# Forming the product of a row's minimum score and the row's scale on the scalar engine instead of the vector engine

## The chip, the cores and the metric

The kernel runs on one core of one Trainium2 chip. The metric is the device time of one execution in microseconds, lower is better. Three timed executions of the kernel before gave 1954.22, 1947.15 and 1951.80 us, median 1951.8 us. The engines are named as the profile names them: PE is the matrix engine (PEld its weight loads), DVE the vector engine, ACT the scalar engine, POOL the GpSimd engine, SP the queue that issues DMAs. Each engine works through its own instructions in the order in which they stand, and waits for the others through semaphores.

## The reference, cut to what matters

Two layers of a trunk over 512 latent tokens and 256 context tokens, D_MODEL 1024, all in float32. Each layer projects the normalised tokens, runs two kinds of attention (a 2-D neighbourhood attention with 8 heads, and a grouped-query attention with 8 query heads over 2 key heads), merges the two branches with gates, and runs a gated feed-forward block. The change touches the softmax of the grouped-query attention alone, and there the query's own normalisation:

```
def rms_norm(x, g):
    xf = x.astype(jnp.float32)
    y = xf * lax.rsqrt(jnp.mean(xf * xf, axis=-1, keepdims=True) + EPS)
    return (y * g.astype(jnp.float32)).astype(x.dtype)

qb = apply_rope(rms_norm(heads(gq, GQA_Q_HEADS), q_gain[l]), cos, sin)
kb = apply_rope(rms_norm(heads(gk, GQA_KV_HEADS), k_gain[l]), cos, sin)

def softmax_attn(q, k, v):
    s = jnp.einsum('bgrqd,bgkd->bgrqk', q, k).astype(jnp.float32) * SCALE
    p = jax.nn.softmax(s, axis=-1).astype(v.dtype)
    return jnp.einsum('bgrqk,bgkd->bgrqd', p, v)
```

## The kernel before, in words

Every float32 product is done in three passes of a faster number format: each operand is split into a high and a low part (high by a copy on ACT, low by a subtraction on DVE or POOL), and PE multiplies high by high, high by low and low by high. So nearly every tile costs ACT and DVE an operation each, and PE three matmuls.

The query is not normalised before its scores are formed. The scores come out of PE with the sign turned (QSCALE is negative), and the factor 1/rms of a query row, `r`, is applied inside the softmax: the exponential is exp(nr * s + m), where `nr` is -r (one number a row) and `m` is r times the smallest (most negative) score of the row. So the softmax needs three steps before its exponential: the smallest score of each row (L1048, a reduction on DVE over 768 scores), its product with `r` (L1054), and the exponential on ACT with `m` as bias and `nr` as scale (L1056), which also sums the row. Behind it DVE takes the reciprocal of the sum (L1009) and scales the row (L1010). PE then turns the probabilities (tile `tp`, L1066), ACT and DVE split them (`pth` L1016, `ptl` L1017), PE multiplies them with the values (tile `y`, L1076), and ACT and DVE join its two halves (`ys` L1024, L1027).

`gqa_pair` makes an item of one head and two blocks of 128 queries: `scores` for both, then `soft` for both, then `exp` for both, then three calls of `turn`, then `values`. There are 16 such items in each layer, 64 softmaxes of 128 rows by 768 keys in all. `ctx_item` does the same for the context queries (layer 0 only): two blocks side by side, 256 keys each; for the grouped-query heads (8 of 16) it forms the products of both blocks at L1098.

What sets the order. In the attention part PE's order is written out by a planner, `Flow`: it keeps a clock of PE and a line of booked time for ACT ("a"), DVE ("v") and POOL ("g"). `go` books an operation at the first gap of its engine's line, at fixed rates (table RATE: an "a" operation 0.06 us and 0.00083 us a column, a "v" operation 0.065 us and 0.00105 us a column, times a factor of the layer), and returns when its result is there. The items are PE's main thread; between their steps, while a result is not yet due, the planner lets PE work on fillers: the projections that are still to be done (tile `pj`, L384, and `pv`, L957). When a `turn` may stand in PE's order is what `go` returned for its `exp`. The scores have one PSUM buffer for an item (`sc`, one of three banks), so the next item's scores wait for both exponentials; `tp` and `y` share three banks. The order on ACT, DVE, POOL and SP is set by a scheduler that follows its own model of times, with PE's order as given.

Of the kernel before, what the change touches and what calls it, by code (L numbers as in the profile page):

```python
# [14 lines left out]
AF = mybir.ActivationFunctionType  # L15
ALU = mybir.AluOpType
# [9 lines left out]
T = S + CTX  # L26
# [308 lines left out]
class Trunk:  # L335
# [694 lines left out]
    def gqa_pair(self, head, q, kk, val, out, i, pool, done=None):  # L1030

        nc = self.nc
        qt, r, nr, v = q
        ps_, pts = [], []

        def scores(s, b):

            for lo, up in ((0, S), (S, T)) if b % 2 == 0 else ((0, 256), (256, T)):
                for k in range(2):
                    nc.tensor.matmul(  # L1040
                        s[:, lo:up], qt[:, b * P : (b + 1) * P], kk[k][:, lo:up],
                        start=(k == 0 and (b % 2 == 0 or lo > 0)), stop=(k == 1), skip_group_check=True)

        ms = {}

        def soft(s, b, at):
            m = ms[b] = pool.tile([P, 2], F32, tag="m", bufs=4, name=self.name("m"))
            nc.vector.tensor_reduce(m[:, 0:1], s[:, :T], axis=AX.X, op=ALU.min)  # L1048
            return self.go(("v", T), at=at)

        def exp(s, b, at):
            m = ms[b]
            c = 2 * b + v
            nc.vector.tensor_tensor(m[:, 0:1], m[:, 0:1], r[:, c : c + 1], op=ALU.mult)  # L1054
            p = pool.tile([P, T], F32, tag="p", name=self.name("p"))
            nc.scalar.activation(p, s[:, :T], AF.Exp, bias=m[:, 0:1], scale=nr[:, c : c + 1], accum_out=m[:, 1:2])  # L1056
            self.soften(p, m[:, 1:2], pool)
            ps_.append(p)
            end = self.go(("v", 1), ("e", T), at=at)
            return end, self.go(("v", 1), ("w", T), at=end)  # L1060

        def turn(k):
            tp = self.ps("t", "tp")
            for b in range(2):
                for j in range(2):
                    nc.tensor.transpose(  # L1066
                        tp[:, (2 * j + b) * P : (2 * j + b + 1) * P], ps_[b][:, (k + j) * P : (k + j + 1) * P], self.ident)
            pts.append(self.split_t(tp, pool))
            return self.go(("a", S), ("v", S), at=self.flow.clock + 4 * PASS)

        def values():
            y = self.ps("b", "y")
            for hl in range(2):
                for k in range(6):
                    j = k % 2
                    nc.tensor.matmul(  # L1076
                        y[:, 0:256], val[:, k * P : (k + 1) * P], pts[k // 2][hl][:, j * 256 : (j + 1) * 256],
                        start=(hl == 0 and k == 0), stop=(hl == 1 and k == 5))
            return self.join(y, out, head, [(0, 256, 256 * i)], pool)

        return Item(
            [(lambda s, b=b: scores(s, b), lambda s, at, b=b: soft(s, b, at), lambda s, at, b=b: exp(s, b, at))
             for b in (2 * i, 2 * i + 1)], T,
            [lambda k=k: turn(k) for k in (0, 2, 4)], [values],
            (2 * T * COL, 4 * PASS, 12 * 256 * COL), done)

    def ctx_item(self, head, score, val, out, r, nr, v, pool, done):

        nc = self.nc
        ps_, pts = [], []  # L1090

        def soft(s, at):
            m = pool.tile([P, 4], F32, tag="mc", bufs=4, name=self.name("m"))
            nc.vector.tensor_reduce(
                m[:, 0:2], s[:, 0:512].rearrange("p (a b) -> p a b", a=2), axis=AX.X, op=ALU.min)
            if r is not None:
                rr = r[:].rearrange("p (t v) -> p v t", v=2)[:, v, 4:6]
                nc.vector.tensor_tensor(m[:, 0:2], m[:, 0:2], rr, op=ALU.mult)  # L1098
            p = pool.tile([P, 512], F32, tag="p", name=self.name("p"))
            for b in range(2):  # L1100
                c = slice(b * 256, (b + 1) * 256)
                scale = -1.0 if nr is None else nr[:, 8 + 2 * b + v : 9 + 2 * b + v]
                nc.scalar.activation(
                    p[:, c], s[:, c], AF.Exp, bias=m[:, b : b + 1], scale=scale, accum_out=m[:, 2 + b : 3 + b])
                self.soften(p[:, c], m[:, 2 + b : 3 + b], pool)
            ps_.append(p)
            end = self.go(("v", S), ("v", 1), ("e", 256), ("e", 256), at=at)
            return end, self.go(("v", 1), ("v", 1), ("w", 256), ("w", 256), at=end - 0.5)

        def turn():  # L1110
            p = ps_[0]
            tp = self.ps("t", "tp")
            for k in range(2):
                for b in range(2):
                    nc.tensor.transpose(
                        tp[:, (2 * k + b) * P : (2 * k + b + 1) * P],
                        p[:, b * 256 + k * P : b * 256 + (k + 1) * P], self.ident)
            pts.append(self.split_t(tp, pool))
            return self.go(("a", S), ("v", S), at=self.flow.clock + 4 * PASS)

        def values():
            y = self.ps("b", "y")
            for hl in range(2):
                for k in range(2):
                    nc.tensor.matmul(
                        y[:, 0:256], val[:, (4 + k) * P : (5 + k) * P], pts[0][hl][:, k * 256 : (k + 1) * 256],
                        start=(hl == 0 and k == 0), stop=(hl == 1 and k == 1))
            return self.join(y, out, head, [(0, 256, S)], pool)

        return Item([(score, soft)], 512, [turn], [values], (4 * 256 * COL, 4 * PASS, 4 * 256 * COL), done)  # L1130

    def gqa_ctx(self, head, q, kk, val, out, pool, done=None):
# [1225 lines left out]
```

## Time and profile before

| What | Value |
|---|---|
| median of three timed runs | 1951.8 us (1947.15 to 1954.22) |
| the profiled execution | 1945.29 us, its span 1943.5 us, so 1.79 us around the span |
| busy share of the span | PE 98%, PEld 91%, DVE 76%, ACT 49%, POOL 12% |
| granted PE clock, mean | 0.998 of full speed |
| the exponentials of the items in layer 0 | 97 to 264 us of the span |
| the exponentials of the items in layer 1 | 1193 to 1316 us of the span |

A matmul's row in the trace is longer than its share of PE, since matmuls overlap: what PE needs for one is the distance between two starts. PE is at work in nearly all of the span, so time can be lost or won only where PE stands idle or runs at a lower clock, and the views that tell this are the waits of PE and the busy time by stretch.

### The profile page before, as it was taken

Reading aid. Unit: us, or ns where it says so; the run is one execution under the profiler, and the core shown is the slowest. Engines: PE = TensorE matmul, PEld = TensorE weight load, DVE = VectorE, ACT = ScalarE, POOL = GpSimd, SP = SyncE. Lnnn points to the kernel's source line nnn. Section 1 sums busy time; section 2 is a strip of 40 time slices with the busy share of each in tenths; the row PEclk is TensorE's granted clock in tenths of the full one; section 3 lists DMA queues with packets and bytes.
Section 4 is the critical chain, followed back from the end, with each engine's and each line's share of the span. In section 5 each row is a group of like instructions: output and inputs, shape, how many; then the busy total and the mean of one; then the engine's idle time right before and its main releaser. Section 6 shows DMA issues by size and latency. Waiting matters only on the chain.

```text
span 1943.5 us, 31493 instructions
## 1 busy us (share of the span) xinstructions
PE 1912.1 (98%) x12298; PEld 1775.8 (91%) x12298; DVE 1470.0 (76%) x2802; ACT 943.0 (49%) x1822; POOL 226.6 (12%) x131
## 2 busy tenths in 40 slices
PE   8999999999999999999999998999999999999998
PEld 8989999998899999999999888889988999999998
DVE  7468887769877888786868577888657687877785
ACT  5466666652336533342424346666553355544553
POOL 0332222213300000000000012322300000000000
PEclk9999999999999999999999999999999999999999
DMA  8121112235562233334344411112235532332332
GB/s 328 44 65 48 47 64 63 77 105 182 170 217 87 66 120 122 117 116 133 131 141 143 143 62 55 47 60 64 73 102 173 201 109 77 98 120 88 103 97 83
DMA packets 71669, 210.85 MB, mean 108 GB/s; under 512 B 8544, under 2 KB 10720, under 8 KB 71520
## 3 DMA queue, kind: packets, MB, share of 16 engines
q1 hardware_dynamic: 71520, 208.84, 33.5%
q8 instruction: 96, 1.57, 0.3%
q14 instruction: 53, 0.43, 0.1%
HBM read 196.75 MB, written 6.82 MB: 105 GB/s over the span
## 4 chain that ended last, share of the span: by engine, by line
PE 69%; DVE 4%; issue 1%; ACT 1%; POOL 0%; DMA 0%; DVEq 0%; POOLq 0%; ACTq 0%
PE po L384 21%; PE qu L1740 14%; PE pj L384 11%; PE qv L1740 7%; PE pp L384 4%; PE qc L1740 3%; PE pf L384 3%; PE pv L957 1%; PE sc L1040 1%; PE y L1076 1%; PE tp L1066 1%; PE y L1203 1%; PE sc L1167 1%; PE tp L1191 1%; DVE m L1048 0%
## 5 line engine op out<-in xcount | busy, mean ns | idle before, releaser
L1740 PE MATMUL qu<-r,w 128*128 128x384 f32 (+1 forms) x1872 | 295.9, 310 | 0.3
L1740 PEld LDWEIGHTS qu<-r,w 128*128 128x128 f32 x1872 | 281.0, 190 | 4.9 <-DVE tt L2219 3.7
L384 PE MATMUL pj<-h,wh 128*128 128x512 f32 (+1 forms) x704 | 257.4, 366 | 3.3 <-ACT kg L816 1.7
L384 PE MATMUL pj<-h,wl 128*128 128x512 f32 (+1 forms) x704 | 247.6, 352 | 1.2 <-POOL wl L371 1.2
L384 PE MATMUL pj<-hl,wh 128*128 128x512 f32 (+1 forms) x704 | 247.0, 351 | 0.0
L369 ACT ACTIVATE wh<-wr 128x1024 fp32r<-128x1024 f32 (+1 forms) x131 | 124.6, 954 | 168.9 <-issue 43.5
L1603 ACT ACTIVATE w<-wr 128x512 fp32r<-128x512 f32 x234 | 145.4, 625 | 107.6 <-DVE wr L2183 36.1
L384 PE MATMUL po<-ph,wh 128*128 128x512 f32 (+1 forms) x576 | 197.5, 343 | 0.0
L384 PE MATMUL po<-ph,wl 128*128 128x512 f32 (+1 forms) x576 | 196.9, 342 | 0.0
L384 PE MATMUL po<-pl,wh 128*128 128x512 f32 (+1 forms) x576 | 196.3, 341 | 0.0
L371 POOL TENSOR_TENSOR wl<-wr,wh 128x1024 fp32r<-128x1024 f32 (+1 forms) x67 | 151.0, 2258 | 370.8 <-ACT wh L369 364.7
L1595 DVE SCALAR_TENSOR_TENSOR x<-po,G,x 128x256 f32<-128x256 f32 (+3 forms) x168 | 99.2, 596 | 101.0 <-PE po L384 100.0
L1607 DVE TENSOR_TENSOR w<-wr,w 128x512 fp32r<-128x512 f32 x234 | 159.4, 686 | 11.9 <-ACT w L1603 11.0
L384 PEld LDWEIGHTS pj<-h,wl 128*128 128x128 f32 x704 | 133.3, 189 | 19.7 <-POOL wl L371 1.6
L1740 PE MATMUL qv<-r,w 128*128 128x384 f32 (+1 forms) x936 | 150.7, 310 | 0.3 <-ACT tt L1746 0.3
L384 PEld LDWEIGHTS pj<-h,wh 128*128 128x128 f32 x704 | 133.7, 190 | 17.4 <-ACT kg L816 1.9
L384 PEld LDWEIGHTS pj<-hl,wh 128*128 128x128 f32 x704 | 134.0, 190 | 13.5
L1740 PEld LDWEIGHTS qv<-r,w 128*128 128x128 f32 x936 | 141.2, 190 | 0.5 <-ACT tt L1746 0.5
L1016 ACT ACTIVATE pth<-tp 128x512 fp32r<-128x512 f32 x176 | 103.2, 595 | 65.1 <-PE tp L1066 36.8
L512 POOL TENSOR_TENSOR rs<-rs,expo 128x2 f32<-128x2 f32 (+2 forms) x8 | 6.2, 773 | 1100.4 <-DVE rs L511 1100.4
L1017 DVE TENSOR_TENSOR ptl<-tp,pth 128x512 fp32r<-128x512 f32 x176 | 119.4, 684 | 18.4 <-ACT pth L1016 17.0
L384 PEld LDWEIGHTS po<-ph,wl 128*128 128x128 f32 x576 | 108.3, 188 | 14.3 <-DVE wl L1911 0.4
(255 smaller groups left out, 4325.2 us busy)
## 6 DMA issues: line engine op xcount, KB each, us to landing
wr<-wfi SPq DMA_DIRECT2D x88, 512.0 KB, 3.3
wr<-wmodT SPq DMA_DIRECT2D x84, 512.0 KB, 3.4
wr<-win SPq DMA_DIRECT2D x68, 512.0 KB, 3.3
wr<-wfo SPq DMA_DIRECT2D x64, 256.0 KB, 2.7
wr<-wo SPq DMA_DIRECT2D x26, 512.0 KB, 3.9
wr<-wp SPq DMA_DIRECT2D x32, 256.0 KB, 3.0
x<-x SPq DMA_DIRECT2D x16, 384.0 KB, 6.7
wr<-wmod SPq DMA_DIRECT2D x12, 512.0 KB, 7.6
```

The lines of the kernel that those rows point to most:

```text
L369: nc.scalar.activation(hi, raw, AF.Copy)
L371: (eng or nc.gpsimd).tensor_tensor(lo, raw, hi[:].bitcast(F32), op=ALU.subtract)
L384: nc.tensor.matmul(ps[:, : b - a], u[:, c], v[k][:, a:b], start=(k == 0 and i == 0), stop=(k == nk - 1 and i == 2),)
L957: nc.tensor.matmul(ps[:, t * 256 : t * 256 + 256], a[k][:, tok], b[:, c], start=(k == 0 and i == 0), stop=(k == KB - 1 and i == 2))
L1016: nc.scalar.activation(hi, tp, AF.Copy)
L1017: nc.vector.tensor_tensor(lo, tp, hi[:].bitcast(F32), op=ALU.subtract)
L1040: nc.tensor.matmul(s[:, lo:up], qt[:, b * P : (b + 1) * P], kk[k][:, lo:up], start=(k == 0 and (b % 2 == 0 or lo > 0)), stop=(k == 1), ski ...
L1066: nc.tensor.transpose(tp[:, (2 * j + b) * P : (2 * j + b + 1) * P], ps_[b][:, (k + j) * P : (k + j + 1) * P], self.ident)
L1595: self.nc.vector.scalar_tensor_tensor(x[j][:, f:u], ps[:, f - a : u - a], self.G[l][i][:, s, j : j + 1], x[j][:, f:u], op0=ALU.mult, op1=A ...
L1603: self.nc.scalar.activation(t[:, :n], src, AF.Copy)
L1607: self.nc.vector.tensor_tensor(t[:, n : 2 * n], src, t[:, :n].bitcast(F32), op=ALU.subtract)
L1740: nc.tensor.matmul(banks[bank], u[:, c], v, start=(first and k == 0 and i == 0), stop=(k == kn - 1 and i == 2), skip_group_check=True)
```

## The change

At two places the small product moves from DVE to ACT. In `exp` one multiplication of a column of 128 numbers becomes one ACT activation (a copy with the row's scale as factor). In `ctx_item` one DVE multiplication of two columns becomes two ACT activations of one column. In `exp` the planner's booking of one column changes from "v" to "a"; the booking in `ctx_item` stays.

```
-            nc.vector.tensor_tensor(m[:, 0:1], m[:, 0:1], r[:, c : c + 1], op=ALU.mult)
+            nc.scalar.activation(m[:, 0:1], m[:, 0:1], AF.Copy, scale=r[:, c : c + 1])
             p = pool.tile([P, T], F32, tag="p", name=self.name("p"))
             nc.scalar.activation(p, s[:, :T], AF.Exp, bias=m[:, 0:1], scale=nr[:, c : c + 1], accum_out=m[:, 1:2])
...
-            end = self.go(("v", 1), ("e", T), at=at)
+            end = self.go(("a", 1), ("e", T), at=at)
             return end, self.go(("v", 1), ("w", T), at=end)
...
-                nc.vector.tensor_tensor(m[:, 0:2], m[:, 0:2], rr, op=ALU.mult)
+                for b in range(2):
+                    nc.scalar.activation(m[:, b : b + 1], m[:, b : b + 1], AF.Copy, scale=rr[:, b : b + 1])
```

DVE has 72 instructions fewer (64 and 8), ACT 80 more (64 and 16). The number of ACT's table loads is four as before, and DMAs are as many as before. Because the planner books another line, orders change too, all of it inside the two attention stages; behind them each engine has the instructions of before in the order of before.

On ACT, in layer 0, around the exponentials of the second item (first the order before: `pth` are high parts of turned probabilities, `qh` high parts of a projection, `p` the exponentials):

```order
L1016 ACTIVATE pth_1078<-tp_1073 128x512
L1016 ACTIVATE pth_1087<-tp_1082 128x512
L1016 ACTIVATE pth_1096<-tp_1091 128x512
L990 ACTIVATE qh_1103<-pj_1026 64x448
L1056 ACTIVATE p_1062,m_1057<-sc_1048,m_1057,nr_778 128x768
L1056 ACTIVATE p_1068,m_1059<-sc_1048,m_1059,nr_778 128x768
```

The same place on ACT with the change:

```order
L1016 ACTIVATE pth_1078<-tp_1073 128x512
L1054 ACTIVATE m_1057<-m_1057,hr_775 128x1
L1016 ACTIVATE pth_1087<-tp_1082 128x512
L1016 ACTIVATE pth_1096<-tp_1091 128x512
L1056 ACTIVATE p_1062,m_1057<-sc_1048,m_1057,nr_778 128x768
L1054 ACTIVATE m_1059<-m_1059,hr_775 128x1
L990 ACTIVATE qh_1103<-pj_1026 64x448
L1056 ACTIVATE p_1068,m_1059<-sc_1048,m_1059,nr_778 128x768
```

The first product stands two copies ahead of its exponential, the second between the two exponentials with a copy of a projection behind it, which stood ahead of both before.

On PE, in layer 0, the third turn of the same item (its exponentials are p_1062 and p_1068) beside a projection that fills PE's time; a piece of the difference:

```order
 L384 MATMUL pj_1212<-h_127,wl_1024 128x512
+L1066 MATMUL tp_1225<-ident_sb,p_1062 128x128 x2
+L1066 MATMUL tp_1225<-ident_sb,p_1068 128x128 x2
 L384 MATMUL pj_1212<-h_129,wh_1022 128x512
 L384 MATMUL pj_1212<-hl_130,wh_1022 128x512
 L384 MATMUL pj_1212<-h_129,wl_1024 128x512
-L1066 MATMUL tp_1228<-ident_sb,p_1062 128x128 x2
-L1066 MATMUL tp_1228<-ident_sb,p_1068 128x128 x2
```

The turn stands three matmuls of a filler earlier. Counted over both layers, 61 of the items' 96 turns stand behind fewer columns of projections than before, by up to 9216 columns (18 matmuls of 512), two behind more, and the rest as before.

On DVE, in layer 1, around the reductions of the item whose scores follow the first evacuation of a key projection `k` there (the order before):

```order
L1017 TENSOR_TENSOR ptl_13250<-tp_13244,pth_13249 128x512
L936 TENSOR_TENSOR k_13321<-pj_13168,k_13321 64x512
L1048 TENSOR_REDUCE m_13271<-sc_13262 128x1
L1048 TENSOR_REDUCE m_13273<-sc_13262 128x1
L936 TENSOR_TENSOR k_13324<-pj_13168,k_13324 64x512
L1054 TENSOR_TENSOR m_13271<-m_13271,hr_12267 128x1
L1017 TENSOR_TENSOR ptl_13293<-tp_13287,pth_13292 128x512
L1054 TENSOR_TENSOR m_13273<-m_13273,hr_12267 128x1
L1027 TENSOR_TENSOR y_13221<-y_13296,ys_13309 64x256
```

The same place on DVE with the change:

```order
L1017 TENSOR_TENSOR ptl_13332<-tp_13326,pth_13331 128x512
L936 TENSOR_TENSOR k_13338<-pj_13245,k_13338 64x512
L936 TENSOR_TENSOR k_13341<-pj_13245,k_13341 64x512
L1048 TENSOR_REDUCE m_13367<-sc_13358 128x1
L1048 TENSOR_REDUCE m_13369<-sc_13358 128x1
L1017 TENSOR_TENSOR ptl_13389<-tp_13383,pth_13388 128x512
L1027 TENSOR_TENSOR y_13198<-y_13392,ys_13405 64x256
```

The two products are gone from the queue, and the low parts of `k` now stand together ahead of both reductions that follow them; `ptl` stands behind the reductions as before.

## Rows read from the trace of the kernel before

**Rows 1.** The page's busy time: us, share of the span, instructions.
```profile
PE 1912.1 (98%) x12298; PEld 1775.8 (91%) x12298; DVE 1470.0 (76%) x2802; ACT 943.0 (49%) x1822; POOL 226.6 (12%) x131
```

**Rows 2.** By stretch: length, busy us of PE, PEld, DVE, ACT, POOL; clock, DMA.
```profile
94.00:200.00 106.00, 104.17 (x691) 94.41 (x690) 79.31 (x170) 65.39 (x133) 31.13 (x14) 1.00 0.17 52
200.00:300.00 100.00, 100.00 (x693) 92.22 (x692) 86.09 (x180) 66.49 (x139) 23.05 (x14) 1.00 0.19 58
300.00:416.00 116.00, 114.32 (x843) 107.30 (x842) 83.87 (x225) 70.63 (x176) 26.61 (x16) 1.00 0.25 75
1190.00:1320.00 130.00, 123.57 (x809) 110.05 (x808) 103.76 (x220) 83.96 (x163) 30.84 (x17) 0.99 0.13 40
1320.00:1440.00 120.00, 119.56 (x843) 110.52 (x842) 87.27 (x220) 71.43 (x160) 32.79 (x19) 1.00 0.26 77
```

**Rows 3.** PE's waits over the span: total us, times, longest us.
```profile
PE sc L1040 <- ACT p L1056: 2.0, 2, 1.7
PE tp L1066 <- DVE ptl L1017: 1.9, 1, 1.9
...
PE y L1076 <- DVE ptl L1017: 1.6, 3, 0.8
...
PE tp L1066 <- DVE p L1010: 0.8, 1, 0.8
```

**Rows 4.** Lines 1054 and 1098: min/median/max ns, and who waited for L1054.
```profile
L1054 DVE TENSOR_TENSOR m<-m,hr x64: 140/150/2060, 97.0 to 1315.5; 128x1 f32<-128x1 f32 x64
...
  ACT p L1056: 21.1, 18
...
L1098 DVE TENSOR_TENSOR m<-m,hr x8: 147/157/1886, 129.4 to 271.7; 128x2 f32<-128x2 f32 x8
```

**Rows 5.** ACT's groups by shape: busy us, mean ns, idle before.
```profile
L990 ACT ACTIVATE qh<-pj 64x64 fp32r<-64x64 f32 x16 | 3.4, 215 | 3.2 <-DVE ql L991 3.0
...
L815 ACT ACTIVATE sq<-pj 128x256 f32<-128x256 f32 x6 | 2.2, 370 | 0.0
...
L816 ACT ACTIVATE qg<-pj,qgain 128x256 f32<-128x256 f32 x4 | 1.9, 474 | 0.0
```

**Rows 6.** Timeline, layer 0's second item: start us, us, engine, line, operation.
```profile
104.30 1.82 DVE L1048 TENSOR_REDUCE m<-sc 128x1 f32<-128x768 f32 x2 [1.47 <-PE sc L1040]
...
105.65 0.39 PE L384 MATMUL pj<-hl,wh 128*128 128x512 f32 x1
...
105.88 0.40 PE L384 MATMUL pj<-h,wl 128*128 128x512 f32 x1
...
106.11 1.28 DVE L1017 TENSOR_TENSOR ptl<-tp,pth 128x512 fp32r<-128x512 f32 x2
...
107.31 0.15 DVE L1054 TENSOR_TENSOR m<-m,hr 128x1 f32<-128x1 f32 x1
...
107.72 0.98 ACT L1056 ACTIVATE p<-sc,m,nr 128x768 f32<-128x768 f32 x1
...
109.42 0.62 DVE L1010 TENSOR_SCALAR p<-p,rc 128x768 f32<-128x768 f32 x1
...
110.37 0.60 PE L1066 MATMUL tp<-ident_sb,p 128*128 128x128 f32 x4
```

**Rows 7.** Timeline, layer 1's first item.
```profile
1189.34 1.81 DVE L1048 TENSOR_REDUCE m<-sc 128x1 f32<-128x768 f32 x2
...
1191.30 1.28 ACT L1056 ACT_TABLE_LOAD   x1 [5.45 <-DVE m L1054]
...
1194.87 0.50 PE L1040 MATMUL sc<-kk,q 128*128 128x512 f32 x1 [1.67 <-ACT p L1056]
```

**Rows 8.** Timeline, layer 1, PE's longest wait between items.
```profile
1284.69 0.66 PE L1066 MATMUL tp<-ident_sb,p 128*128 128x128 f32 x4 [1.91 <-DVE ptl L1017]
```

**Rows 9.** The stretch behind that wait, as rows 2.
```profile
1286.00:1288.00 2.00, 2.00 (x10) 1.80 (x9) 1.64 (x4) 0.49 (x1) 0.00 (x0) 0.50 0.00 0
```

**Rows 10.** Waits of all engines, POOL's for the neighbourhood bias buffers.
```profile
POOL bias L1491 <- DVE m L1178: 50.5, 6, 14.7
```

## The prediction

> **What bounds the kernel now.** I read the page's busy times first. PE is at work in 98% of the span, DVE in 76% [rows 1]: the matmuls bound the kernel, and the change leaves every one of them in place, so it can only add or remove time in which PE stands still. Next I read the attention stages by stretch, since the products run from 97.0 to 1315.5 us [rows 4] and the orders differ only inside the two attention stages. The length of a stretch less PE's busy time is what PE lacks there: 1.8, 0, 1.7, 6.4 and 0.4 us, together 10.4 us [rows 2]. DVE is the next busiest engine there (79.3 of 106, 86.1 of 100, 103.8 of 130 us where the grouped-query items run), ACT is third (65.4, 66.5 and 84.0) [rows 2]. Then PE's waits: for the exponential 2.0 us in two waits, for `ptl` 1.9 us in one, for `ptl` ahead of `y` 1.6 us in three, for the scaled row 0.8 us in one [rows 3]. No wait of PE names the product itself. ACT's does: it waited 21.1 us in 18 waits for L1054 [rows 4], but nearly all of that lies beside PE's fillers. Last I read one item in the timeline, to see what distance there is between a softmax and the turn that needs it.
>
> **What goes from DVE.** 64 products of 150 ns and 8 of 157 ns [rows 4]: 9.6 + 1.3 = 10.9 us of DVE time. On the path it is worth far less, since PE waits for DVE in so few places. What each product also costs is its place in the queue. In the second item both reductions end at 104.30 + 1.82 = 106.12 us, and the second product starts only at 107.31, because two `ptl` subtractions, a merged 1.28 us that begins at 106.11, stand ahead of it; its exponential starts at 107.72 [rows 6].
>
> **What comes to ACT.** 80 activations of one column with a scale taken from a tile. The trace shows none. Nearest is a copy of 64x64 at 215 ns; 256 columns take 370 ns, so a column costs (370 - 215) / 192 = 0.8 ns and one column alone about 215 - 51 = 164 ns. A scale taken from a tile costs 474 - 370 = 104 ns [rows 5]. The estimate is 164 + 104 = 268 ns, with bounds of 150 (no dearer than on DVE) and 215 + 104 = 319 ns. I take 0.27: 80 x 0.27 = 21.6 us of ACT time (12.0 to 25.5). ACT has idle time for it: in 130 us of layer 1 it was busy for 84.0 [rows 2], and 32 products there add 8.6.
>
> The Trainium skill, "ScalarE: Activation LUTs", section "What ACT_TABLE_LOAD costs", gives an ACTIVATE 186 ns and 0.833 ns a column, and about 93 ns more for each operand of one column. That is 280 ns here as an estimate, and the 104 ns of the row agree with its 93; by it the ACT term would be 22.4 us. It speaks against the change: the product is nearly twice as dear on ACT. The same section says that ACTIVATEs back to back overlap by about 93 ns; an exponential that waits for a product on its own engine would lose that, 64 x 0.093 = 6.0 us more of ACT, which no run here shows yet.
>
> **How long a softmax takes.** On the path of one item the first product needs the first reduction alone, which ends near 104.30 + 0.91 = 105.21 us, and no longer stands behind the second. ACT's work from there is two products and two exponentials of 0.98 us, 2.5 us, to near 107.7 us, and the reading of the first row sums, which no row here prices. Before, the second exponential started at 107.72 and lasted 0.98, to 108.70 [rows 6]. The gain is under 1.0 us; I take half of it, so I expect the last exponential of an item up to 0.5 us earlier where ACT is free, and 0.3 to 0.6 us later where ACT has a queue, since the two products then lengthen it by 2 x 0.27.
>
> **What PE's order does with it.** The planner thinks the softmax shorter, and 61 of 96 turns stand behind fewer columns of projections, up to 18 matmuls of 512. Two such matmuls start 105.88 - 105.65 = 0.23 us apart [rows 6], so a turn comes up to 4.1 us earlier in the order; the same projections stand later, and none is lost. The usual shift at one item is three matmuls, 0.7 us. The distance that covers it was 110.37 - (109.42 + 0.62) = 0.33 us at one of the narrowest places [rows 6]. So about as much is taken from the cover as the softmax may win: I value this at 0, with bounds of +8 us (4.1 us lost once in each layer) and -3 us (the waits for the exponential and for the scaled row go, 2.0 + 0.8).
>
> **The two places where something must go.** Layer 1's first item: both reductions end at 1191.15, the products end near 1191.3, ACT's table load of 1.28 us starts there, and PE's next scores wait 1.67 us for the exponentials [rows 7]. With the product on ACT, the load can follow the first product, some 0.6 us after the first reduction's end at 1190.25, and the wait shrinks by about 0.5 us. The wait of 1.91 us for `ptl` at 1284.69 [rows 8]: its queue on DVE loses a product of 0.15 us and has another order; I take half of it as gone, 1.0 us. Behind this wait the granted clock was 0.50 for the 2 us from 1286 [rows 9], the 1.2 GHz level, with PE never idle in that stretch: at least 1 us more, of which I take half too. The other waits on DVE in rows 3, three and one, lose a product of 0.15 us each, 0.6 us. In the other direction 0.3 us for each of the two waits for the exponential, 0.6 us.
>
> **The sum.** -0.5 - 1.0 - 0.5 - 0.6 + 0.6 + 0 = -2.0 us against the profiled execution's 1945.29 us, which is 1943.3. The median of the runs shown is 1951.8, 6.5 us above the profiled execution, and the three runs lie 7.1 us apart; I carry the difference over: 1951.8 - 2.0 = 1949.8, rounded to 1950. About 0.5%, or 9.8 us, is what a measurement of this kernel can tell from no change, and the sum is well inside.
>
> **Rivals.** First, slower: PE is made to wait at the turns. The planner books a product on ACT at 0.06 us and a bit, and the product takes 0.27 and holds up the copies behind it; with turns moved forward, every item whose distance is under 0.7 us lets PE stand. For it speak the 0.33 us above and that ACT's order puts a product ahead of two `pth` copies, so that these wait for a reduction. Against it speaks the shorter way of the first exponential. Priced at 0.35 us for each of 32 items, 11.2 us, and one more drop of the clock at 1 us or more: 12.2 us, about 1964. It decides once half the items wait.
>
> Second, faster beyond the bound: DVE's queue is what makes PE late everywhere, and 10.9 us less of it clears nearly all stalls. All of 10.4 us and 1 us of clock would give 1951.8 - 11.4 = 1940.4. For it speaks that three of the four groups of waits name DVE [rows 3]; against it that 72 short instructions leave DVE at over three quarters of the stretch, and that a part of the waits lies where no item runs.
>
> Third, slower by another way: POOL. In layer 0 POOL's bias buffers waited 50.5 us in six waits of up to 14.7 us [rows 10], low parts of weights stand behind them in the same queue, and the new order puts two bias loads in a row ahead of one such weight. If one weight comes late by a full wait, 14.7 us, it gives 1951.8 + 14.7 = 1966.5; PE's waits of rows 3 show none of this kind now, so the cover was there.
>
> That the change doesn't do what it says can be left out: the order shows the products on ACT. They stand in front of the exponential, not always right in front.
>
> **Chances.** Forecast, within 0.5%: 0.70. PE waits at turns: 0.14. POOL: 0.04. DVE's relief beyond the bound: 0.12. So faster 0.12, same 0.70, slower 0.18. The likeliest case has its own range from its bounds, 1951.8 - 2.0 - 3 to 1951.8 - 2.0 + 8: 1946.8 to 1957.8. For 8 in 10 I widen it toward the rivals on both sides, which lie at 1940.4 and 1964 to 1966.5, about two thirds of the way: 1941 to 1962.
>
> **What would show it.** Right: DVE busy 10 to 11 us less, ACT 18 to 26 us more, L1054 on ACT at 0.2 to 0.32 us, PE's busy time unchanged, its gaps in the five stretches between 6 and 14 us in total, the wait ahead of layer 1's second item near 1.2 us. Wrong: waits of PE at L1066 for L1010 or at L1040 for L1056 in many items, more half-clock stretches in 190 to 270 or 1190 to 1320 us, a wait for `wl` of L371 between 290 and 330 us, or an exponential that starts more than 0.3 us after its product's end.

## The result and the profile after

The changed kernel took 1959.67 us (median of five runs, 1956.91 to 1960.03), the kernel before 1950.45 us in the same comparison: ratio 1.0049, 95% interval 1.0027 to 1.0071. In a second comparison it was 1955.57 against 1950.24 us, ratio 1.0036 (1.0024 to 1.0048). It is slower, by 5 to 9 us. I had forecast no change, 1950 us. That 1959.67 still lies between my 1941 and 1962 is owed to the widening toward the rivals, not to the forecast.

The first view is the page's busy time [rows 1], then the stretches of [rows 2]. Those of layer 1 are moved by 11 us, since that stage starts 11 us later.

```profile
PE 1917.1 (98%) x12298; PEld 1779.0 (91%) x12298; DVE 1461.2 (75%) x2730; ACT 959.9 (49%) x1902; POOL 228.2 (12%) x131
```

```profile
94.00:200.00 106.00, 103.04 (x666) 93.15 (x666) 74.41 (x145) 69.41 (x157) 31.01 (x13) 0.98 0.17 52
200.00:300.00 100.00, 99.27 (x683) 90.52 (x682) 79.06 (x163) 70.25 (x159) 25.56 (x15) 1.00 0.19 58
300.00:416.00 116.00, 114.88 (x851) 108.16 (x851) 83.26 (x223) 70.90 (x174) 26.57 (x16) 1.00 0.22 64
1201.00:1331.00 130.00, 122.20 (x779) 109.05 (x778) 99.23 (x183) 88.45 (x190) 31.29 (x17) 0.96 0.13 40
1331.00:1451.00 120.00, 119.56 (x850) 110.79 (x848) 87.12 (x222) 72.93 (x163) 32.83 (x19) 1.00 0.26 77
```

DVE has 8.8 us less work and ACT 16.9 us more. PE's gaps in the five stretches are 3.0, 0.7, 1.1, 7.8 and 0.4 us, together 13.0 against 10.4. That alone is 2.6 us. The other part is the column of the granted clock: 0.98 and 0.96 in the first and the fourth stretch, where it was 1.00 and 0.99. PE's waits [rows 3] show where the gaps are:

```profile
PE sc L1040 <- ACT p L1056: 5.0, 5, 1.8
...
PE po L384 <- DVE wl L371: 3.4, 2, 2.7
PE y L1076 <- DVE ptl L1017: 3.1, 2, 1.8
...
PE tp L1066 <- DVE p L1010: 1.8, 2, 1.4
```

Scores wait for the exponential 5.0 us in five waits (2.0 in two before). `y` waits 3.1 us for `ptl` (1.6), and the 1.91-us wait of a turn for `ptl` is gone. The product on ACT (line 1054, [rows 4]):

```profile
L1054 ACT ACTIVATE m<-m,hr x64: 278/285/298, 96.9 to 1329.9; 128x1 f32<-128x1 f32 x64
```

**Stage by stage.** I cut the span at PE's first score and the last `y` of the neighbourhood attention of each layer. Of 14.6 us between the two profiled spans, layer 0's attention has 4.2, layer 1's 3.7, the merge and output projection of layer 0 7.1, all other stages together less than 0.5 us. Two more profiles of the changed kernel give 4.2 and 4.4 for layer 0, 1.0 and 0.6 for layer 1: attention is 7.8, 5.2 and 5.0 us longer.

Two things make up these numbers: PE's idle time in the two stages (length less busy time: before 11.8 us; changed 14.4, 14.4 and 14.6) and the half-clock stretches, as in [rows 9]. Such a stretch is one in which the granted clock was 0.50. Before has one of them in the attention stages, 3.4 us long, in each of two profiles; at half speed that costs 1.7 us, as an estimate. The changed kernel has 13.6 us at half speed in the first profile, 6.8 in each of the other two. 14.4 - 11.8 + (13.6 - 3.4) / 2 = 7.7 us, measured 7.8; for the second profile 14.4 - 11.8 + 1.7 = 4.3, measured 5.2; for the third 14.6 - 11.8 + 1.7 = 4.5, measured 5.0. So the account is good to about 1 us. The idle time comes back within 0.2 us from profile to profile of one kernel; the number of half-clock stretches does not.

Here is what stood ahead of one such stretch (timeline, layer 0: DVE and PE, then the window behind it):

```profile
170.06 1.82 DVE L1048 TENSOR_REDUCE m<-sc 128x1 f32<-128x768 f32 x2
171.92 0.95 DVE L919 TENSOR_TENSOR q<-qg,q 64x768 fp32r<-64x768 f32 x1
172.90 0.69 DVE L1017 TENSOR_TENSOR ptl<-tp,pth 128x512 fp32r<-128x512 f32 x1
...
173.74 0.36 PE L1076 MATMUL y<-pth,v 128*128 128x256 f32 x1 [1.76 <-DVE ptl L1017]
```

```profile
174.50:176.50 2.00, 2.00 (x11) 2.00 (x10) 1.72 (x3) 0.58 (x3) 2.00 (x2) 0.50 0.17 29
```

`ptl` starts only at 172.90, behind two reductions and a `q`; PE stands 1.76 us, and behind that the clock is 0.50. The kernel before at the same item:

```profile
170.46 0.94 DVE L1048 TENSOR_REDUCE m<-sc 128x1 f32<-128x768 f32 x1
171.43 0.69 DVE L1017 TENSOR_TENSOR ptl<-tp,pth 128x512 fp32r<-128x512 f32 x1
172.04 0.95 DVE L1048 TENSOR_REDUCE m<-sc 128x1 f32<-128x768 f32 x1
...
172.27 0.36 PE L1076 MATMUL y<-pth,v 128*128 128x256 f32 x1 [0.58 <-DVE ptl L1017]
```

There `ptl` stood between the two reductions. No product is in either piece: the scheduler laid DVE's queue out anew, as it does in every version below, so no run moves a product and nothing else.

### The profile page after: what moved, and what is told of

Read it like the earlier page. It is cut to its first block, busy times and chain, and to the rows that moved or that the text cites. A ratio compares the mean times of both kernels' runs of the same rounds, so it can differ in the third digit from the quotient of the medians.

```text
span 1958.1 us, 31483 instructions
## 1 busy us (share of the span) xinstructions
PE 1917.1 (98%) x12298; PEld 1779.0 (91%) x12298; DVE 1461.2 (75%) x2730; ACT 959.9 (49%) x1902; POOL 228.2 (12%) x131
## 4 chain that ended last, share of the span: by engine, by line
PE 64%; DVE 4%; ACT 2%; issue 1%; DMA 1%; POOL 0%; SPq 0%; DVEq 0%; POOLq 0%; ACTq 0%
PE po L384 20%; PE qu L1741 14%; PE pj L384 8%; PE qv L1741 7%; PE qc L1741 3%; PE pf L384 3%; PE pp L384 2%; PE pv L957 2%; PE sc L1040 1%; PE y L1076 1%; PE tp L1066 1%; PE y L1204 1%; PE sc L1168 1%; PE tp L1192 1%; ACT p L1056 0%
## 5 line engine op out<-in xcount | busy, mean ns | idle before, releaser
L1608 DVE TENSOR_TENSOR w<-wr,w 128x512 fp32r<-128x512 f32 x234 | 159.1, 684 | 11.2 <-ACT w L1604 10.2
L384 PEld LDWEIGHTS pj<-hl,wh 128*128 128x128 f32 x704 | 133.7, 190 | 13.6
```

What stands on the lines that cost most here:

```text
L384: nc.tensor.matmul(ps[:, : b - a], u[:, c], v[k][:, a:b], start=(k == 0 and i == 0), stop=(k == nk - 1 and i == 2),)
L1608: self.nc.vector.tensor_tensor(t[:, n : 2 * n], src, t[:, :n].bitcast(F32), op=ALU.subtract)
```

## The experiments

Theories at the start: A, the planner's moved turns cost the time; B, the product on ACT costs it; C, much of it is scatter in layer 0's merge. "Attention" below is the length of both stages against the first profile of before.

**Booking and place apart.** e1 is the changed kernel booked as before (PE's order of before). e2 is the kernel before booked as changed (PE's order of the changed kernel), with all products on DVE, those of `ctx_item` too:

```
e1 (against changed)  -            end = self.go(("a", 1), ("e", T), at=at)
                      +            end = self.go(("v", 1), ("e", T), at=at)
e2 (against before)   -            end = self.go(("v", 1), ("e", T), at=at)
                      +            end = self.go(("a", 1), ("e", T), at=at)
```

> The products are on the scalar engine in both places, and the planner books the product on the line 'v' as in the kernel before, so PE's and SP's orders are those of before. Theory A (the planner's moved turns cost the time): the extra PE waits for the exponential and for the scaled row and the half-clock stretches go, time within 3 us of before, about 1950 us. Theory B (the product itself on the scalar engine, by its length or its place, costs the time): it stays slow, about 1959 us, with PE waits of the changed kernel. Theory C (the 7 us in the merge of layer 0 are scatter of weight loads, and the attention's part is small): about 1952 to 1956 us, with the merge of layer 0 as long as it happens to be, not tied to the order.

> The products stay on the vector engine as in the kernel before, and only the planner's booking is changed to the line 'a', so PE's, POOL's and SP's orders are those of the changed kernel. Theory A (moved turns): slow, about 1957 to 1960 us, PE's waits for the exponential 4 to 5 us in all and two or more half-clock stretches inside the attention stages. Theory B (the product on the scalar engine): about 1950 us, PE's waits as before. Theory C (scatter of the merge): between the two, attention stages within 3 us of before.

e1: 1948.03 us, ratio 0.9991 (0.9979 to 1.0004), attention -0.8 us, no half-clock stretch in it. e2: 1950.78, 0.9996 (0.9984 to 1.0008), attention +2.9, two stretches. Neither half of the change is slow alone: A fails on e2, and B, as it stood, on e1.

**Second profiles of both kernels.**

> The kernel before once more, for a second profile of it. If the merge and output projection of layer 0 scatter by run (theory C), that stretch here differs by several us from the first profile of before. If not, every stage is within 1 us of it, and the 7 us of the changed kernel there are a consequence of the change (theories A and B).

> The changed kernel once more, for a second profile of it. Theories A and B: the attention stages again 4.2 and 3.7 us longer than before's (within 1.5 us) with the half-clock stretches at the same items, near 174, 1205 and 1277 us. Theory C: the merge of layer 0 differs from the first profile of the changed kernel by several us.

Before again: attention within 0.1 us, half-clock stretch at the same place, but the merge 5.3 us longer, with a wait that the first profile does not have:

```profile
PE po L384 <- DVE wl L371: 2.5, 1, 2.5
```

So C holds in part: the first profile of before, on which the prediction was built, was an execution without this wait. The changed kernel again: attention +5.2, merge +5.7; layer 1 lacks two of its three lots of 3.4 us at half clock and is 1.0 us longer than before's, not the 3.7 within 1.5 that theories A and B had expected. Its merge is 1.4 us off the first profile's, less than the several that C had expected.

The changed kernel was timed and profiled a third time beside e12 to e14 (the second comparison above). If the merge is late by scatter, I had expected two groups of runs, near 1951 to 1954 and 1956 to 1960 us; if the change makes it late each time, all of them in 1956 to 1961. The five runs lie at 1955.2 to 1955.6 and 1958.4 to 1959.2 us: this tells neither.

**The first exponential.** In the changed kernel it does not start when its product is done (timeline, layer 1):

```profile
1274.40 1.82 DVE L1048 TENSOR_REDUCE m<-sc 128x1 f32<-128x768 f32 x2 [0.92 <-PE sc L1040]
...
1275.39 0.30 ACT L1054 ACTIVATE m<-m,hr 128x1 f32<-128x1 f32 x1
...
1276.32 0.99 ACT L1056 ACTIVATE p<-sc,m,nr 128x768 f32<-128x768 f32 x1 [0.63 <-DVE m L1048]
```

The product ends at 1275.69, both reductions at 1276.22, the exponential starts 0.1 us later. In none of the 32 items of this kernel, of before or of the versions below does one start before the second reduction's end. The Trainium skill, "PSUM — Partial Sum Buffer", section "PSUM bank collisions raise a hardware error", says that two engines must not be in one bank of PSUM at once, reads included, and that software has to keep them apart. The two blocks' scores lie side by side in 1536 columns of three banks and share the middle one. e8 cuts the second reduction:

```
+            if b % 2 == 0:
                 nc.vector.tensor_reduce(m[:, 0:1], s[:, :T], axis=AX.X, op=ALU.min)
+            else:
+                nc.vector.tensor_reduce(m[:, 0:1], s[:, 0:256], axis=AX.X, op=ALU.min)
+                nc.vector.tensor_reduce(m[:, 1:2], s[:, 256:T], axis=AX.X, op=ALU.min)
+                nc.vector.tensor_tensor(m[:, 0:1], m[:, 0:1], m[:, 1:2], op=ALU.min)
```

> The changed kernel with the second block's reduction cut in two (first its columns 0 to 255, which lie in the same PSUM bank as the end of the first block's scores, then the rest) and a vector minimum of both. PE's order is that of the changed kernel. The vector engine has 128 instructions more. Theory D (the first exponential is held until the vector engine has finished reading the shared bank): the first exponential of an item starts near the end of the first part of the second reduction, about 0.6 us ahead of the end of the last part, as soon as its product is done. Theory E (it is held until the last reduction, or by something else that comes then): it starts 0.1 us after the last reduction's end as in the changed kernel. The time of the kernel is not what this run is for: the additional vector work may make it up to 5 us longer.

```profile
1279.19 0.41 DVE L1051 TENSOR_REDUCE m<-sc 128x1 f32<-128x256 f32 x1
1279.30 0.30 ACT L1059 ACTIVATE m<-m,hr 128x1 f32<-128x1 f32 x1 [0.37 <-DVE m L1049]
1279.53 0.67 DVE L1052 TENSOR_REDUCE m<-sc 128x1 f32<-128x512 f32 x1
1280.29 0.99 ACT L1061 ACTIVATE p<-sc,m,nr 128x768 f32<-128x768 f32 x1 [0.69 <-DVE m L1052]
```

Theory E: the exponential waits for the last part too (to 1280.20), though that part reads another bank. So the Trainium skill's rule can account for the wait to 1279.60 only. What is left points to a dependence of the program on the tile as a whole; that is inferred, no run splits the tile. (One run, 1961.49 us, attention +8.9.)

**The product's length.** A second activation of one column behind each product, in either order of PE:

```
             nc.scalar.activation(m[:, 0:1], m[:, 0:1], AF.Copy, scale=r[:, c : c + 1])
+            nc.scalar.activation(m[:, 0:1], m[:, 0:1], AF.Copy)
```

> The changed kernel with a second activation of one column behind each of the 64 products of the pairs (a copy of the product onto itself, about 0.2 us), so the way from reduction to exponential on the scalar engine is 0.2 us a softmax longer; orders of PE as in the changed kernel, in which the turns stand earlier. Theory A2 (neither the product nor the moved turns cost alone, but both together: the moved turns left no cover for the longer softmax): the two attention stages become longer than in the changed kernel by 2 to 8 us, with more waits of PE for the scaled row and for the exponential. Theory B2 (the product's length is hidden, the loss is from order alone): attention within 1 us of the changed kernel plus one half-clock stretch (1.7 us) at most.

> The same doubled product, but the planner books it on the line 'v' as in the kernel before, so PE's order is that of before, with the turns later. Theory A2: the cover of that order hides the doubled product too, attention within 2 us of before and of the kernel with a single product and this booking, time about 1948 to 1952 us. Theory B2 (order alone) expects the same here; a loss of over 4 us in attention would speak against both and for the product's length on the scalar engine as such (theory B).

e9: 1969.8 us, 1.0115 (1.0093 to 1.0137), attention +15.3. e10: 1961.06, 1.0072 (1.0046 to 1.0098), attention +10.8, where A2 had expected 2 us at most: PE's order of before does not cover it either. PE's scores wait for the exponential 11.2 and 8.5 us. So 0.2 us more on ACT's way to an exponential is paid in both orders; this speaks for theory B, at twice the length. That one product was already at the edge of the cover is my reading of it.

**One product for both blocks**, on DVE, behind the second reduction (the lines that form it; the edit also gives both blocks one tile `m`):

```
+                rr = r[:].rearrange("p (t v) -> p v t", v=2)[:, v, b - 1 : b + 1]
+                nc.vector.tensor_tensor(m[:, 0:2], m[:, 0:2], rr, op=ALU.mult)
```

> The kernel before with one vector multiplication of two columns for both blocks of an item, right behind the second reduction, in place of two of one column: 32 vector instructions fewer, the planner's bookings and PE's order as before. Since the first exponential does not start before the second reduction's end in the kernel before either, it loses nothing, and the second exponential's product no longer stands behind other vector work. Theory D or E: the second exponential starts about 1.0 us after the first in nearly all items (before: 1.0 to 1.5, once 2.8), the scaled row is up to 0.5 us earlier, waits of PE for ptl or the exponential shrink by 0 to 2 us; time 1948 to 1952 us, attention stages 0 to 3 us shorter than before. If the second product's place in the vector queue costs nothing: no difference in the attention stages beyond one half-clock stretch, 1.7 us.

A miss: 1957.98 us, 1.005 (1.003 to 1.007), attention +7.0. The exponentials do stand 0.98 us apart, but the first now starts 1.52 us (mean) behind the second reduction, against 0.77 before: the one product waits in DVE's queue, and both exponentials wait for it. Most of the 4.4 us of idle time that it adds to before's is one wait in layer 0, of `y` at 177.69: 4.0 us, where before waits 0.58.

**One block's product at a time.** e12 has the first block's product on ACT and the second's on DVE (its edit is shown), e13 the mirror, both booked as before; e14 has both on ACT, ahead of both exponentials, booked as before too. In all three the products of `ctx_item` stay on ACT:

```
+            if b % 2 == 0:
                 nc.scalar.activation(m[:, 0:1], m[:, 0:1], AF.Copy, scale=r[:, c : c + 1])
+            else:
+                nc.vector.tensor_tensor(m[:, 0:1], m[:, 0:1], r[:, c : c + 1], op=ALU.mult)
```

> Only the product of an item's first block is on the scalar engine; that of the second block stays on the vector engine; booking 'v', so PE's order is that of before. Theory F (what decides is when the last exponential of an item ends after the second reduction, and the changed kernel loses because the second product stands on the scalar engine between the two exponentials): the first exponential starts near 0.4 us after the second reduction's end as in the changed kernel (before: 0.77, mean), the second about 1.3 us behind it as before, so its end lies 2.7 us after the reduction (before 3.07, changed 3.24); attention stages without half-clock stretches 0 to 3 us shorter than before, time 0 to 4 us below the kernel with both products on the scalar engine and the same booking. Theory B (each product on the scalar engine costs by its length): half of the loss of that kernel, within 1 us of before.

> The mirror of the run above: the product of the first block stays on the vector engine, that of the second is on the scalar engine; booking 'v', PE's order as before, the same number of instructions on each engine as in the mirror. Theory F: the first exponential starts as late as before (0.77 us after the reduction, mean), the second is put off by its product to 1.5 to 1.85 us behind it, the last exponential ends 3.3 to 3.6 us after the reduction; more waits of PE's scores for the exponential than in the mirror, attention 2 to 6 us longer than there. Theory B: as long as the mirror, within 1 us apart from half-clock stretches.

> Both products on the scalar engine as in the changed kernel, but issued behind the reductions, so both stand ahead of the first exponential and none between the two; booking 'v', PE's order as before. Theory F: the first exponential starts 0.3 us later than with the product between (about 0.6 to 0.7 us after the reduction), the second 1.0 to 1.3 us behind it, the last one ends at about the same time as with the product between (3.1 to 3.3 us); attention within 2 us of that kernel apart from half-clock stretches. If the place between the exponentials cost in itself (its wait and the read of the row's sum), the last end comes 0.2 us earlier and attention shrinks by about 3 us.

e12: 1946.71 us, ratio 0.9974 (0.9964 to 0.9983): faster than both kernels. Attention -3.9, no half-clock stretch. e13: 1956.25, 1.0034 (1.002 to 1.0048), attention +6.3, three stretches. e14: 1954.18, 1.0019 (1.0007 to 1.0031), attention +5.0 with idle time of 12.4 us, near before's, and 13.6 us at half clock. e12 and e13 have the same instructions on each engine; only the block differs. PE's waits of e12 and of e13 (the names' lines are 3 further):

```profile
PE sc L1040 <- ACT p L1059: 1.9, 2, 1.6
...
PE tp L1069 <- DVE ptl L1017: 1.6, 1, 1.6
...
PE y L1079 <- DVE ptl L1017: 0.4, 2, 0.3
```

```profile
PE sc L1040 <- ACT p L1059: 2.4, 2, 1.9
PE st L804 <- DVE y L1027: 2.3, 1, 2.3
PE tp L1069 <- DVE ptl L1017: 1.9, 1, 1.9
...
PE y L1079 <- DVE hr L806: 1.6, 1, 1.6
```

The end of the last exponential behind the second reduction (mean of 32 items) is 3.07 us before, 3.24 changed, 2.83 in e12, 2.99 in e13 and 2.72 in e14. So theory F named the right product, but not the whole way: by this measure alone e13 and e14 should have gained. It had expected 1.5 to 1.85 us between the exponentials of e13, and the mean is 1.10: in none of its 32 items does the second product stand between them (28 in the changed kernel, 27 in e1). Both products stand ahead, and what the exponentials then put off are the copies behind them. The copy `ys` stands between them in 3 items of e13 and in 2 of e14, against 12 of before. One item of e13 (layer 1):

```profile
1269.78 0.98 ACT L1059 ACTIVATE p<-sc,m,nr 128x768 f32<-128x768 f32 x1
...
1270.88 0.38 ACT L1024 ACTIVATE ys<-y 64x256 f32<-64x256 f32 x1
...
1271.74 0.42 DVE L1027 TENSOR_TENSOR y<-y,ys 64x256 f32<-64x256 f32 x1
...
1272.21 1.06 PE L804 MATMUL st<-hones,sq 128*128 128x2 f32 x7 [2.25 <-DVE y L1027]
```

Before waits 0.68 us there, with `ys` between the exponentials. e14 waits 2.16 us there, and both wait 1.58 us for `hr` at `y` in layer 0. What remains of e13's loss is nearly all the clock, 3.4 us.

**The better version in the changed order of PE**, and the planner told the product's true length:

```
e16  (e12)        end = self.go(("a", 1), ("e", T), at=at)
e3   +RATE = dict(m=(0.285, 0.0, "a"), ...
     +            end = self.go(("m", 1), ("e", T), at=at)
```

> The first block's product on the scalar engine, the second's on the vector engine (the version that came out below before), but booked on the line 'a', so PE's order is that of the changed kernel. Theory G (the moved turns and the second product on the scalar engine each take cover, and the loss is their sum at a few places): between the version with booking 'v' (attention 3.9 us shorter than before) and the changed kernel (5.0 to 7.8 us longer): attention 0 to 3 us longer than before, its stalls of PE over 0.65 us 11 to 13 us in total. Theory H (with the shorter way the moved turns are harmless): attention within 1.7 us of the version with booking 'v'.

> The changed kernel with the planner told the measured length of the product, 0.285 us on the line 'a' in place of 0.06. PE's order is a third one. Theory G: the turns get cover back; attention 0 to 4 us longer than before, below the changed kernel; stalls of PE 11 to 14 us. If the booking's line rather than its length did it (the line 'a' has room where 'v' is full), it stays at the changed kernel's 5 to 8 us.

e16: 1948.55 us, 0.9985 (0.997 to 1.0), attention -1.1. It is the changed kernel with the second block's product put back on DVE, and 6 to 9 us of attention are gone with that. Both expectations are missed: G had attention 0 to 3 us longer than before, H within 1.7 us of e12, and it lies 2.8 us from e12. By idle time alone H holds: e12 has 9.4 us, e16 9.8, and two half-clock stretches make up the difference. e3 is a miss of both expectations: 1967.96 us, 1.0087 (1.0073 to 1.0101), attention +17.3, with single waits of 3.2 us for an exponential. A truer length for one step did not give a better order.

**Does a later attention make the merge late?** Five score passes of the first block issued twice:

```
+            self.nsc = getattr(self, "nsc", 0) + 1
+            for _ in range(2 if self.nsc in (5, 11, 15, 19, 25) else 1):
                 for lo, up in ...
```

> The kernel before with the score matmuls of the first block issued twice in five items of layer 0 (20 additional matmuls, about 0.8 us each time, 3.9 us of PE in all; the second pass writes the same numbers), nothing else changed: the attention of layer 0 ends about 4 us later without a change in the softmax. Theory C (the merge's 5 us come and go by themselves): its runs fall into two groups as those of before do, near 1948 to 1951 and 1953 to 1958 us. Theory I (an attention stage that ends later makes the merge late each time): all runs lie in 1953 to 1958 us, and the profile has the merge of layer 0 5 to 7 us longer.

Not settled: 1953.92 us, 1.0017 (1.0007 to 1.0027), merge +5.3 in the profile, but runs from 1951.65 to 1957.95 without a gap between groups.

## Why the prediction was wrong

PE's idle time in the two attention stages, with the product's engine for the first and the second block:

| first / second | booked "v" | booked "a" |
|---|---|---|
| DVE / DVE | 11.8 (before) | 12.8 (e2) |
| ACT / ACT | 11.7 (e1) | 14.4 (changed) |
| ACT / DVE | 9.4 (e12) | 9.8 (e16) |
| DVE / ACT | 14.6 (e13) | not run |

The first block's product on ACT saves 2.4 to 3.0 us (e12 against before, e16 against e2, e1 against e13). The second block's costs 2.3 to 4.6 (e1 against e12, changed against e16, e13 against before). The moved turns alone cost 0.4 to 1.0; with both products on ACT 2.7. Only before and e2 have the products of `ctx_item` on DVE; in layer 1, which has none, the same differences have the same signs (1.3 to 2.5 saved, 0.2 to 2.5 paid). All but before and changed rest on one profile.

The second product's price is not paid at one place. In the changed order of PE it is paid at the scores: their waits for the exponential are 5.0 us in the changed kernel and 1.9 in e2 and in e16, which have PE's order in common with it (first e2, then e16):

```profile
PE sc L1040 <- ACT p L1056: 1.9, 2, 1.7
PE sc L1040 <- ACT p L1059: 1.9, 2, 1.6
```

In the order of before the scores wait 2.2 us in e1 and 1.9 in e12, and e1 has one wait of 1.63 us at `y` in layer 0 that e12 lacks. In e13 it is paid behind the exponentials, as shown. So the loss of the changed kernel takes both halves of the change: turns that stand earlier, and a second product on ACT. What no run separates is the product from the new order of its neighbours: besides the products, e16 has 96 of DVE's and 80 of ACT's instructions at other places in the queue than the changed kernel.

**"How long a softmax takes" is the step that failed.** I let ACT start when the first reduction ends and expected the last exponential of an item up to 0.5 us earlier. The first exponential is held to the second reduction's end. It does start earlier than before (0.40 us behind that end, mean, against 0.77), but the second product stands behind it, and the distance between the exponentials grows from 1.31 to 1.85 us; so the last one ends 0.17 us later, not up to 0.5 earlier. In the sum I had 0.6 us for waits of the scores for the exponential; they grew by 3.0. Where nothing else stands between, the product adds 0.32 us: in the item above the second exponential starts at 1277.61, 1.29 us behind the first, where 0.97 is the least distance without a product. The rest goes with copies: 44 stand between the two exponentials of an item in the changed kernel, counted over 32 items, and 19 in before. The longest of the scores' waits, but for the one with the table load, is seen in this item (timeline of the changed kernel, layer 1):

```profile
1229.34 0.99 ACT L1056 ACTIVATE p<-sc,m,nr 128x768 f32<-128x768 f32 x1
...
1230.33 0.28 ACT L1054 ACTIVATE m<-m,hr 128x1 f32<-128x1 f32 x1
1230.51 0.58 ACT L1016 ACTIVATE pth<-tp 128x512 fp32r<-128x512 f32 x1
1230.99 1.05 ACT L369 ACTIVATE wh<-wr 128x1024 fp32r<-128x1024 f32 x1
1231.94 0.27 ACT L966 ACTIVATE v<-pv 128x128 fp32r<-128x128 f32 x1
1232.09 0.99 ACT L1056 ACTIVATE p<-sc,m,nr 128x768 f32<-128x768 f32 x1
...
1233.23 0.51 PE L1040 MATMUL sc<-kk,q 128*128 128x512 f32 x1 [1.35 <-ACT p L1056]
```

Three copies stand between the second product and its exponential, and PE's next scores, which need the one score buffer, wait 1.35 us. The same item of e12:

```profile
1220.93 1.00 ACT L1059 ACTIVATE p<-sc,m,nr 128x768 f32<-128x768 f32 x1
...
1221.91 0.27 ACT L966 ACTIVATE v<-pv 128x128 fp32r<-128x128 f32 x1
1222.07 0.60 ACT L1016 ACTIVATE pth<-tp 128x512 fp32r<-128x512 f32 x1
1222.55 1.00 ACT L1059 ACTIVATE p<-sc,m,nr 128x768 f32<-128x768 f32 x1
...
1223.70 0.51 PE L1040 MATMUL sc<-kk,q 128*128 128x512 f32 x1 [0.30 <-ACT p L1059]
```

**"What goes" and "what comes"** were near: DVE -8.8 (I had -10.9), the product 0.288 us (0.27). The 80 products sum to 23.0 us (21.6); ACT's busy time grew by 16.9 only, since rows of ACT overlap. The overlap with the exponential is lost, as I had it: where one stood right behind its own product, it started 0.03 us behind the product's end.

**"What PE's order does with it"**, valued at 0 with +8 as a bound, had the right bound for the wrong reason: the turns cost little by themselves (0.9996 for e2). **The table load**: I expected it behind the first product and a wait of PE near 1.2 us. The product ended at 1201.66, the load started at 1202.24, 0.1 us behind the second reduction's end like the exponentials, and PE's scores waited 1.80 us (before 1.67 [rows 7]). **The 1.91-us wait** [rows 8] went entirely, of which I took half; but two waits for `ptl`, at `y`, came instead, 1.76 and 1.38 us. They need no second product: e2 and e16, with the same order of PE, wait 1.46 and 1.38 us at the same two matmuls. **The clock**: I counted half of one drop as won; the changed kernel has three or two such stretches. I priced idle time and left the clock behind it nearly out: -0.5 us in the sum, while it is 1.7 to 5.1 us of the loss.

**The first rival** had the mechanism nearest to what happened, waits at the turns and a product that holds up copies, at 12.2 us. Its point of decision was wrong: not half the items wait, some five do, each for over a microsecond. **The carry-over** of 6.5 us from profile to median was right as arithmetic; the second profile of before shows late weights as a part of it. **The range**: 1941 lies nine tenths of the way to the rival at 1940.4, not the two thirds that I named; two thirds would be 1942.5.

**The signs.** PE's gaps (13.0 us) and the product's length came out as named for "right", DVE's and ACT's busy times just outside, the wait ahead of layer 1's second item at 1.80 for 1.2. Of those for "wrong", the exponential came more than 0.3 us behind its product's end in 28 of 32 first blocks; but e12 has 27 of them and gains, so that sign showed the hold and not the price.

What stays open: whether the changed kernel makes the merge late more often. In its three profiles the merge is 5.7 to 7.1 us longer than in the first profile of before, but the second of before and those of e12 and e16 have 5.1 to 5.3 of it as well, and e1, e2 and e10 have none. And how the clock decides: e1 has two idle times of 1.6 to 1.8 us in attention without a half-clock stretch.

## What to carry to other kernels

Before a step is moved to the engine of its consumer, ask of each instance what stands between it and the consumer in that queue: here the first product was done during a wait that it could not shorten, the second stood between two exponentials or put off the copies behind them, and the same edit won on one and lost on the other. Move one instance of a pair at a time. And when PE is at 98%, price each idle time of over a microsecond with the clock that may follow it.

## What the runs showed of the hardware

- An activation of one column took 0.285 us (median) with a scale from a tile and 0.198 us without (e10's second activation): the operand costs some 0.09 us. The Trainium skill, "ScalarE: Activation LUTs", section "What ACT_TABLE_LOAD costs", gives 186 ns for an activation without such an operand and about 93 ns more for each; both agree.
- Each exponential with a row sum is followed on ACT by a read of the accumulator of 0.19 us, which stands in ACT's queue ahead of the second product.
- In the attention stages the half-clock stretches lasted 3.4 us or twice that, and each began in or soon behind an idle time of PE of over a microsecond (1.38 to 1.91 us in the first profiles of before and of the changed kernel). Not every such idle time was followed by one: e1 has none behind 1.63 and 1.80 us.
